# First modulation of a decoder trunk: half of its width on TensorE, with the condition's column as the stationary operand

## The chip, the core and the metric

The kernel runs on one core of one Trainium2 chip. The metric is the device time of one execution in microseconds; lower is better. A core has TensorE (PE, matrix products, with its weight loads PEld), VectorE (DVE), ScalarE (ACT), GpSimdE (POOL) and SyncE (SP, which issues most transfers). Each engine works through its own instructions in order and waits on semaphores of the others; 16 DMA engines move data between the chip's memory and the on-chip memory. A tile is a buffer of 128 partitions in the on-chip memory; a bank is a buffer of 128 x 512 values into which PE accumulates.

## What is computed

A trunk of two layers. The input x has 512 positions of width 1024, the condition c is one row of width 1024, and everything is in 32-bit floats. Each layer has three sub-layers (a gated feed-forward part, a mixer of attention and convolution, a second feed-forward part), and each of the six is fed by a norm that the condition modulates:

```
mod = (silu(c) @ w_ada[layer] + b_ada[layer]).reshape(b, N_SUB, N_MOD, D_MODEL)
shift = mod[:, :, 0, None, :]
scale = mod[:, :, 1, None, :]
gate = mod[:, :, 2, None, :]

def ada(z, i):
    return _rmsnorm(z, norm_g[layer, i]) * (1.0 + scale[:, i]) + shift[:, i]

x = x + 0.5 * gate[:, 0] * _swiglu(ada(x, 0), ffn_w1[layer, 0], ffn_w2[layer, 0])
...
```

The change touches only the first of these six modulations: shift and scale (2 x 1024 values) of layer 0, sub-layer 0. Nothing of the trunk's large products can start before some of them are there.

## The kernel before

The 1024 values of the width lie on 8 tiles x[0] to x[7] of 128 partitions (width) by 512 columns (positions). A modulation value belongs to one partition of one such tile, so DVE makes them in columns: cb holds silu(c) as a row repeated over all 128 partitions, a weight tile holds 128 rows of the transposed w_ada, and one instruction (ada_job, line 305) multiplies the two, 128 x 1024, and adds up along the row, which leaves 128 values of shift or of scale. For each of the 8 tiles j there is one job for shift and one for scale, 16 in all; ada_norm (lines 311 and 312) adds the bias and multiplies by the norm's gain for one range of tiles.

At the program's start (lines 980 to 1043) cb is made by two PE products of one row of ones with the two halves of c (line 1005) and a Silu on ACT (line 1006). The squares of x are summed (ACT line 403, DVE line 404), reduced by PE (line 410), turned into an inverse root by ten small DVE instructions, and spread over the partitions by four PE transposes (line 419). The result is called rb.

The first feed-forward part has its first eight weight products fed in an order of its own, side_by_side (lines 1019 to 1043). The width's 8 tiles are taken in 4 pairs k = 0 to 3. For a pair, the two jobs of each of its tiles, ada_norm, and then first.early make the first 256 positions (DVE line 438, ACT line 461, and the split into a high and a low half on ACT line 519 and DVE line 520), with which PE makes one step of 24 products (line 286). After k = 1 and k = 3 first.second makes the other 256 positions of two pairs, and PE makes two further steps of 24. That is 8 steps, 192 products of 128 x 128 by 256 columns. They need four weight tiles (raw), which ACT and DVE split into halves whi and wlo (lines 169 and 170). Then come the ordinary groups of the first feed-forward part, which begin with the tile called left.

The order in which an engine takes its instructions is set by a scheduler from the program's order and its priorities, so an instruction can stand earlier or later than the code suggests. Transfers stand in SP's queue in order: one that waits for its buffer holds up those behind it. The weights of this modulation (ada) have three buffers of 1 MB, each for shift and scale of one tile j.

Of the kernel before, what the change touches and what calls it, by code (L numbers as in the profile page):

```python
# [10 lines left out]
F32 = mybir.dt.float32  # L11
# [3 lines left out]
AF = mybir.ActivationFunctionType  # L15
# [93 lines left out]
def trunk(ctx: ExitStack, tc: tile.TileContext, t: dict):  # L109
# [8 lines left out]
    def acc_bank():  # L118
        return psum.tile([128, 512], F32, name="acc", tag="acc", bufs=6)
# [6 lines left out]
    def half_kb(name):  # L126
        return tmp.tile([128, S], F32, name=name, tag="ev", bufs=8)
# [175 lines left out]
    def ada_job(w, l, s, m, j):  # L303
        raw, _ = mods[l, s]
        nc.vector.scalar_tensor_tensor(w, w, 1.0, cb, op0=ALU.mult, op1=ALU.mult,  # L305
                                       accum_out=raw[:, m, j:j + 1])
# [677 lines left out]
    ada = []  # L984

    def load_ada():
        ada.append(sp.tile([128, 2, D], F32, name="ada", tag="ada", bufs=3))
        nc.sync.dma_start(ada[-1], t["w_ada"][0, 0:2 * KD].rearrange("(m j) p n -> j p m n", m=2)[len(ada) - 1])

    c = [half_kb("c")[0:1] for _ in range(2)]  # L990
    for half in range(2):
        nc.sync.dma_start(c[half], t["c"][:, half * 512:half * 512 + 512])
    load_ada()
    for j in range(KD):
        nc.sync.dma_start(x[j], t["xT"][j])
        if j == 3:
            nc.sync.dma_start(ident, t["ident"])
            nc.sync.dma_start(par, t["par"])
    load_ada()
    lead[:] = 0, 0, 0  # L1000
    fetch(4)
    for half in range(2):
        ps = acc_bank()
        cols = slice(half * 512, half * 512 + 512)
        nc.tensor.matmul(ps, row, c[half], start=True, stop=True)
        nc.scalar.activation(cb[:, cols], ps, AF.Silu)
    for m in range(2):
        ada_job(ada[0][:, m], 0, 0, m, 0)
    acc = sums()
    for j in range(KD):  # L1010
        squares(acc, j, slice(0, S))
    load_ada()
    load_ada()
    rb = spread(inv_rms(acc, 4), acc_bank())
    h = new_h()
    first = Blocks(0, 0, h, sp, first_tiles(sp))
    Tail.blocks[:] = [first]
# [1 line left out]
    def side_by_side(banks, done):  # L1019
        plain_groups = _ffn_order()[:4]  # L1020
        feeds = [Feed(0, 0, h, sum(plain_groups[i:i + 2], []), banks) for i in (0, 2)]
        for k in range(KD // 2):
            for j in (2 * k, 2 * k + 1):
                for m in range(2) if j else ():
                    ada_job(ada[j][:, m], 0, 0, m, j)
                if j and len(ada) < KD:
                    load_ada()
            ada_norm(0, 0, slice(2 * k, 2 * k + 2))
            first.early(rb[:, 0:256], k)
            feeds[0].step(k)  # L1030
            if k % 2:
                first.second(rb[:, 256:512], k // 2)
                feeds[1].step(k - 1)
                feeds[1].step(k)
        lead[:] = AHEAD, LOADED, SUMS
        for step in (first.t1, first.t2, first.t3):
            for two in range(2):
                after(LATER, lambda step=step, two=two: step(two))
        for group in plain_groups:
            for n, p in group:  # L1040
                done(n, p)
        release(True)
        late_constants()
# [26 lines left out]
def _laid_out(inp):  # L1070
    c = np.ascontiguousarray
    a = {k: np.asarray(v) for k, v in inp.items()}
    out = {}
    out["c"] = c(a["c"].reshape(1, D))
    out["xT"] = c(a["x"][0].T.reshape(KD, 128, S))
    out["w_ada"] = c(a["w_ada"].transpose(0, 2, 1).reshape(DEPTH, 72, 128, D))
    out["par"] = c(np.concatenate([
        a["b_ada"].reshape(DEPTH * 72, 128).T,
        a["norm_g"].reshape(DEPTH * 3 * KD, 128).T,
        a["conv_w"].reshape(DEPTH, 3, 4, 128).transpose(3, 0, 2, 1).reshape(128, 24),  # L1080
        a["conv_b"].reshape(DEPTH * 4, 128).T], axis=1))
    out["ident"] = np.eye(128, dtype=np.float32)
    out["mask"] = _mask()
    q, k = a["q_norm_g"], a["k_norm_g"]
    out["qkg"] = c(np.stack([q, q, k, k], axis=1).reshape(1, DEPTH * 4 * HD))
    w = a["w_in"]

    qkv = w[:, :, :1536].reshape(DEPTH, 4, 2, 128, 3, 4, 128)
    out["w_qkv"] = c(qkv.transpose(0, 5, 1, 3, 2, 4, 6).reshape(DEPTH, 4, 4, 128, 768))
    gcu = w[:, :, 1536:].reshape(DEPTH, KD, 128, 3, 4, 128)  # L1090
    out["w_gcu"] = c(gcu.transpose(0, 4, 3, 2, 1, 5).reshape(DEPTH, 4, 3, 128, D))
    wo = a["w_out"].reshape(DEPTH, KD, 128, KD, 128)
    wo = np.concatenate([wo[:, 4:], wo[:, :4]], axis=1)
    out["w_out"] = c(wo.transpose(0, 3, 2, 1, 4).reshape(DEPTH, KD, 128, D))

    w1 = a["ffn_w1"].reshape(DEPTH, 2, KD // 2, 2, 128, 2, NP, 2, 128)
    out["w1"] = c(w1.transpose(0, 1, 6, 5, 3, 4, 7, 2, 8).reshape(DEPTH, 2, NP, 4, 128, D))
    w2 = a["ffn_w2"].reshape(DEPTH, 2, NF, 128, KD, 128)
    wa = w2[:, :, :16].reshape(DEPTH, 2, 2, 8, 128, KD, 128)
    out["w2a"] = c(wa.transpose(0, 1, 2, 5, 4, 3, 6).reshape(DEPTH, 2, 2, KD, 128, D))  # L1100
    out["w2b"] = c(w2[:, :, 16:].transpose(0, 1, 4, 3, 2, 5).reshape(DEPTH, 2, KD, 128, 768))
    return out
# [17 lines left out]
```

## Time and profile before

| | us |
|---|---|
| median of three runs | 1890.41 (1887.54 to 1891.17) |
| the profiled execution | 1890.81 |
| its span | 1889.0 |
| PE busy | 1834.2 (97% of the span) |
| DVE busy | 1418.1 (75%) |
| ACT busy | 925.2 (49%) |

The span goes from the first to the last instruction in the profile; 1.8 us of the profiled execution lie outside it. The views used are the page of the whole execution, the timeline of one engine (start, duration, what it is, and in brackets how long the engine had been idle before it and what ended that), and a table of stretches with each engine's busy time.

### The profile page before, as it was taken

Reading aid. Unit: us, or ns where it says so; the run is one execution under the profiler, and the core shown is the slowest. Engines: PE = TensorE matmul, PEld = TensorE weight load, DVE = VectorE, ACT = ScalarE, POOL = GpSimd, SP = SyncE. Lnnn points to the kernel's source line nnn. Section 1 sums busy time; section 2 is a strip of 40 time slices with the busy share of each in tenths; the row PEclk is TensorE's granted clock in tenths of the full one; section 3 lists DMA queues with packets and bytes.
Section 4 is the critical chain, followed back from the end, with each engine's and each line's share of the span. In section 5 each row is a group of like instructions: output and inputs, shape, how many; then the busy total and the mean of one; then the engine's idle time right before and its main releaser. Section 6 shows DMA issues by size and latency. Waiting matters only on the chain.

```text
span 1889.0 us, 31142 instructions
## 1 busy us (share of the span) xinstructions
PE 1834.2 (97%) x12436; PEld 1702.1 (90%) x12436; DVE 1418.1 (75%) x2434; ACT 925.2 (49%) x1462; POOL 81.6 (4%) x156
## 2 busy tenths in 40 slices
PE   5899999999999999999989999999999999999999
PEld 4888999999988998998989999898998899989898
DVE  7887878787866887887778877766977768647564
ACT  3552543446653743543546435354656646436342
POOL 0000000000000000000000000000000000000000
PEclk9999999999999999999999999999999999999999
DMA  8678775522315278787725866723222245626422
GB/s 320 191 225 261 215 241 188 156 76 65 110 67 179 66 206 264 196 244 236 217 68 156 242 207 166 245 71 97 84 73 90 97 127 133 165 83 168 133 61 85
DMA packets 85124, 296.32 MB, mean 157 GB/s; under 512 B 9330, under 2 KB 10354, under 8 KB 84980
## 3 DMA queue, kind: packets, MB, share of 16 engines
q1 hardware_dynamic: 73460, 252.40, 38.9%
q0 software_dynamic: 11520, 41.95, 12.9%
q8 instruction: 97, 1.59, 0.3%
q14 instruction: 47, 0.39, 0.1%
HBM read 292.21 MB, written 2.10 MB: 156 GB/s over the span
## 4 chain that ended last, share of the span: by engine, by line
PE 81%; DVE 5%; ACT 3%; DMA 2%; issue 2%; ACTq 0%; DVEq 0%; POOLq 0%
PE acc L286 35%; PE acc L279 14%; PE acc L280 14%; PE acc L281 14%; DMA left<-in_w 2%; DVE wlo L170 1%; DVE h L520 1%; PE acc L873 1%; ACT whi L169 1%; PE tp L864 1%; PE tp L894 1%; DMA ada<-in_w_ada 1%; PE acc L904 0%; PE acc L905 0%; DVE p L908 0%
## 5 line engine op out<-in xcount | busy, mean ns | idle before, releaser
L286 PE MATMUL acc<-h,whi 128*128 128x256 f32 x4992 | 894.5, 282 | 28.6 <-ACT h L519 16.0
L286 PEld LDWEIGHTS acc<-h,whi 128*128 128x128 f32 x4992 | 770.2, 189 | 35.2 <-ACT h L519 18.0
L286 PE MATMUL acc<-h,wlo 128*128 128x256 f32 x2496 | 700.7, 281 | 0.4 <-DVE wlo L170 0.4
L169 ACT ACTIVATE whi<-raw 128x1024 fp32r<-128x1024 f32 (+1 forms) x304 | 306.0, 1011 | 372.3 <-PE acc L280 242.3
L286 PEld LDWEIGHTS acc<-h,wlo 128*128 128x128 f32 x2496 | 473.6, 190 | 1.1 <-DVE wlo L170 1.0
L170 DVE TENSOR_TENSOR wlo<-raw,whi 128x1024 fp32r<-128x1024 f32 (+1 forms) x304 | 352.5, 1166 | 52.9 <-ACT whi L169 49.9
L279 PE MATMUL acc<-hidh,whi 128*128 128x512 f32 (+1 forms) x776 | 287.4, 370 | 0.0
L281 PE MATMUL acc<-hidh,wlo 128*128 128x512 f32 (+1 forms) x776 | 287.0, 370 | 0.0
L280 PE MATMUL acc<-hidl,whi 128*128 128x512 f32 (+1 forms) x776 | 286.9, 370 | 0.0
L305 DVE SCALAR_TENSOR_TENSOR ada<-ada,cb 128x1024 f32<-128x1024 f32 x144 | 174.0, 1222 | 87.7 <-DMA ada<-in_w_ada 81.6
L536 DVE SCALAR_TENSOR_TENSOR x<-acc,fin,x 128x512 f32<-128x512 f32 (+1 forms) x130 | 87.6, 675 | 128.3 <-PE acc L281 128.1
L281 PEld LDWEIGHTS acc<-hidh,wlo 128*128 128x128 f32 x776 | 146.3, 189 | 24.8
L280 PEld LDWEIGHTS acc<-hidl,whi 128*128 128x128 f32 x776 | 146.4, 189 | 24.3
L279 PEld LDWEIGHTS acc<-hidh,whi 128*128 128x128 f32 x776 | 146.3, 189 | 24.3
L169 ACT ACTIVATE whi<-sum 128x1024 fp32r<-128x1024 f32 x80 | 84.8, 1061 | 147.0 <-DVE sum L222 100.7
L169 ACT ACTIVATE whi<-left 128x1024 fp32r<-128x1024 f32 x80 | 84.7, 1058 | 122.7 <-DMA left<-in_w 79.2
L170 DVE TENSOR_TENSOR wlo<-left,whi 128x1024 fp32r<-128x1024 f32 x80 | 97.7, 1221 | 52.6 <-ACT whi L169 52.1
L279 PE MATMUL acc<-h,whi 128*128 128x512 f32 (+1 forms) x346 | 132.1, 382 | 0.4 <-ACT h L519 0.4
L280 PE MATMUL acc<-h,whi 128*128 128x512 f32 (+1 forms) x346 | 126.9, 367 | 1.0 <-DVE h L520 1.0
L281 PE MATMUL acc<-h,wlo 128*128 128x512 f32 (+1 forms) x346 | 127.0, 367 | 0.0
L170 DVE TENSOR_TENSOR wlo<-sum,whi 128x1024 fp32r<-128x1024 f32 x80 | 97.7, 1221 | 32.5 <-ACT whi L169 32.3
L279 PE MATMUL acc<-whi,h 128*128 128x384 f32 x256 | 89.0, 349 | 4.8 <-ACT h L442 4.8
(123 smaller groups left out, 2148.4 us busy)
## 6 DMA issues: line engine op xcount, KB each, us to landing
ada<-in_w_ada SPq DMA_DIRECT2D x128, 512.0 KB, 4.4
raw<-in_w SPq DMA_DIRECT2D x96, 512.0 KB, 4.3
raw<-in_w2a SPq DMA_DIRECT2D x64, 512.0 KB, 5.0
left<-in_w SPq DMA_DIRECT2D x40, 512.0 KB, 4.4
sum<-in_w SPq DMA_DIRECT2D x40, 512.0 KB, 4.7
sum<-in_w POOLq DMA_DIRECT2D x40, 512.0 KB, 7.0
left<-in_w POOLq DMA_DIRECT2D x40, 512.0 KB, 5.4
raw<-in_w2b SPq DMA_DIRECT2D x32, 384.0 KB, 3.4
```

The source lines that it names most:

```text
L169: nc.scalar.activation(hi, raw, AF.Copy)
L170: nc.vector.tensor_tensor(out=lo, in0=raw, in1=hi.bitcast(F32), op=ALU.subtract)
L279: nc.tensor.matmul(out, a[0], b[0], start=first, stop=False)
L280: nc.tensor.matmul(out, a[0], b[1], start=False, stop=False)
L281: nc.tensor.matmul(out, a[1], b[0], start=False, stop=last)
L286: nc.tensor.matmul(out, p, q, start=first and i == 0, stop=i == 2, skip_group_check=True)
L305: nc.vector.scalar_tensor_tensor(w, w, 1.0, cb, op0=ALU.mult, op1=ALU.mult, accum_out=raw[:, m, j:j + 1])
L520: return nc.vector.tensor_tensor(out=lo, in0=v, in1=hi.bitcast(F32), op=ALU.subtract)
L536: nc.vector.scalar_tensor_tensor(x[j][:, cols], ps, gate, x[j][:, cols], op0=ALU.mult, op1=ALU.add)
L864: nc.tensor.transpose(pt[:, c * 128:(c + 1) * 128], p[:, c * 128:(c + 1) * 128], ident)
L873: nc.tensor.matmul(ps, v[c][:, i], z[:, c], start=c == m == 0, stop=c == n - 1 and m == 1)
L894: nc.tensor.transpose(ps[:, b * 128:(b + 1) * 128], qk[b][:, c], identr)
```

## The change

The weights of tiles 0 to 3 (shift and scale, 4 x 1 MB of ada before) are no longer laid out for DVE. A second layout, w_mod, holds w_ada's first 512 columns of shift and of scale with the condition's index on the partitions: 8 transfers of 128 x 1024, 0.5 MB each. The condition is also loaded as a 128 x 8 tile ccol, on which ACT makes Silu. PE takes one column of ccol as the stationary operand and 512 columns of weights as the moving one, 8 products in a row for scale (m = 1) and 8 for shift (m = 0), each set adding up in one row of 512 values. ACT copies the two rows out, PE turns each piece of 128 values into a column (8 products, line 1034 of the changed program), ACT copies these 8 columns into the modulation's tile, and one ada_norm covers tiles 0 to 3. Tiles 4 to 7 stay with DVE. The new weight tiles have four buffers, two of their own and two of the pool that later modulations use; ada has two buffers in place of three. The load of the four raw tiles stands behind the new loads in the program.

```
     def load_ada():
-        ada.append(sp.tile([128, 2, D], F32, name="ada", tag="ada", bufs=3))
-        nc.sync.dma_start(ada[-1], t["w_ada"][0, 0:2 * KD].rearrange("(m j) p n -> j p m n", m=2)[len(ada) - 1])
+        j = KD // 2 + len(ada)
+        ada.append(sp.tile([128, 2, D], F32, name="ada", tag="ada", bufs=2))
+        nc.sync.dma_start(ada[-1], t["w_ada"][0, 0:2 * KD].rearrange("(m j) p n -> j p m n", m=2)[j])
+    ccol = sp.tile([128, KD], F32, name="ccol")
+    nc.sync.dma_start(ccol, t["ccol"])
...
-    load_ada()
...
+    rows = {}
+    for m in (1, 0):
+        rows[m] = []
+        for k in range(KD // 2):
+            pool, name = ((sp, "adar"), (wp, "ada"))[k % 2]
+            rows[m].append(pool.tile([128, 1024], F32, name=name, tag=name, bufs=2).rearrange("p (i n) -> p i n", i=2))
+            nc.sync.dma_start(rows[m][-1], t["w_mod"][m, k])
+    nc.scalar.activation(ccol, ccol, AF.Silu)
     lead[:] = 0, 0, 0
-    fetch(4)
...
-    for m in range(2):
-        ada_job(ada[0][:, m], 0, 0, m, 0)
...
+    rb = spread(inv_rms(acc, 4), acc_bank())
+    flat = {}
+    for m in (1, 0):
+        ps = acc_bank()[0:1]
+        for k in range(KD):
+            nc.tensor.matmul(ps, ccol[:, k:k + 1], rows[m][k // 2][:, k % 2], start=k == 0, stop=k == KD - 1)
+        flat[m] = half_kb("row")[0:1]
+        nc.scalar.activation(flat[m], ps, AF.Copy)
+    fetch(4)
     load_ada()
     load_ada()
-    rb = spread(inv_rms(acc, 4), acc_bank())
+    ps = tp_bank()
+    for m in (1, 0):
+        for j in range(KD // 2):
+            nc.tensor.matmul(ps[:, m * 4 + j:m * 4 + j + 1], flat[m][:, j * 128:j * 128 + 128], row[:, 0:1],
+                             start=m == 1 and j == 0, stop=True, skip_group_check=True)
+    nc.scalar.activation(mods[0, 0][0][:, 0:2, 0:KD // 2], ps[:, 0:8].rearrange("p (m j) -> p m j", m=2), AF.Copy)
+    ada_norm(0, 0, slice(0, KD // 2))
...
         for k in range(KD // 2):
-            for j in (2 * k, 2 * k + 1):
-                for m in range(2) if j else ():
-                    ada_job(ada[j][:, m], 0, 0, m, j)
-                if j and len(ada) < KD:
-                    load_ada()
-            ada_norm(0, 0, slice(2 * k, 2 * k + 2))
+            if k > 1:
+                for j in (2 * k, 2 * k + 1):
+                    for m in range(2):
+                        ada_job(ada[j - KD // 2][:, m], 0, 0, m, j)
+                    if len(ada) < KD // 2:
+                        load_ada()
+                ada_norm(0, 0, slice(2 * k, 2 * k + 2))
```

PE's instructions from the product with the condition to the first large product, before the change:

```order
L1005 MATMUL acc_135<-c_93,row_82 128x512
L1005 MATMUL acc_138<-c_94,row_82 128x512
L410 MATMUL tp_170<-ones_80,ssq_143 128x1 x4
L419 MATMUL acc_195<-ident_77,sm_193 128x128 x4
L286 MATMUL acc_209<-h_200,whi_119 128x256
L286 MATMUL acc_210<-h_200,whi_127 128x256
```

PE's instructions from the spreading of rb to the first large product, after the change (adar and ada are here the tiles of w_mod):

```order
L419 MATMUL acc_180<-ident_77,sm_178 128x128 x4
L1025 MATMUL acc_185<-adar_109,ccol_93 1x512 x2
L1025 MATMUL acc_185<-ada_111,ccol_93 1x512 x2
L1025 MATMUL acc_185<-adar_113,ccol_93 1x512 x2
L1025 MATMUL acc_185<-ada_115,ccol_93 1x512 x2
L1025 MATMUL acc_196<-adar_117,ccol_93 1x512 x2
L1025 MATMUL acc_196<-ada_119,ccol_93 1x512 x2
L1025 MATMUL acc_196<-adar_121,ccol_93 1x512 x2
L1025 MATMUL acc_196<-ada_123,ccol_93 1x512 x2
L1034 MATMUL tp_235<-row_82,row_194 128x1 x4
L1034 MATMUL tp_235<-row_82,row_205 128x1 x4
L286 MATMUL acc_256<-h_247,whi_215 128x256
```

Between the spreading and the first large product stand now 16 products with the condition and 8 that turn rows into columns.

DVE's instructions from the end of the inverse root to the jobs of the second pair, before the change:

```order
L388 SCALAR_TENSOR_TENSOR sm_193<-sm_191,sm_183 128x4
L305 SCALAR_TENSOR_TENSOR ada_109,mod00_85<-ada_109,cb_67 128x1024 x2
L311 TENSOR_TENSOR fin00_86<-mod00_85,par_76 128x2x2
L312 SCALAR_TENSOR_TENSOR fin00_86<-fin00_86,par_76 128x2
L170 TENSOR_TENSOR wlo_120<-raw_111,whi_119 128x1024
L438 SCALAR_TENSOR_TENSOR z_219<-x1_69,fin00_86,acc_195 128x256
L438 SCALAR_TENSOR_TENSOR z_219<-x0_68,fin00_86,acc_195 128x256
L170 TENSOR_TENSOR wlo_124<-raw_113,whi_123 128x1024
L170 TENSOR_TENSOR wlo_128<-raw_115,whi_127 128x1024
L520 TENSOR_TENSOR h_200<-hva_202,h_200 128x2x256
L170 TENSOR_TENSOR wlo_132<-raw_117,whi_131 128x1024
L305 SCALAR_TENSOR_TENSOR ada_166,mod00_85<-ada_166,cb_67 128x1024 x2
```

The same place after the change:

```order
L388 SCALAR_TENSOR_TENSOR sm_178<-sm_176,sm_168 128x4
L170 TENSOR_TENSOR wlo_216<-raw_207,whi_215 128x1024
L170 TENSOR_TENSOR wlo_220<-raw_209,whi_219 128x1024
L170 TENSOR_TENSOR wlo_224<-raw_211,whi_223 128x1024
L170 TENSOR_TENSOR wlo_228<-raw_213,whi_227 128x1024
L311 TENSOR_TENSOR fin00_86<-mod00_85,par_76 128x2x4
L312 SCALAR_TENSOR_TENSOR fin00_86<-fin00_86,par_76 128x4
L438 SCALAR_TENSOR_TENSOR z_260<-x1_69,fin00_86,acc_180 128x256
L438 SCALAR_TENSOR_TENSOR z_260<-x0_68,fin00_86,acc_180 128x256
L438 SCALAR_TENSOR_TENSOR z_291<-x3_71,fin00_86,acc_180 128x256
L438 SCALAR_TENSOR_TENSOR z_291<-x2_70,fin00_86,acc_180 128x256
```

The jobs of tiles 0 to 3 are gone, all four low halves of the weights stand ahead of the modulation's end (fin), and the first job that is left stands behind the start of pairs 0 and 1.

SP's transfers behind those of x, after the change (raw are the four weight tiles of the first products):

```order
L1009 DMA ada_115<-in_w_mod 128x1024 [waits DMAHW0_49]
L162 DMA raw_207<-in_w1 128x1024 [waits DMAHW1_49]
L162 DMA raw_209<-in_w1 128x1024 [waits DMAHW2_49]
L1009 DMA adar_117<-in_w_mod 128x1024 [waits DMAHW5_49,DMAHW3_49,PE_49]
L1009 DMA ada_119<-in_w_mod 128x1024 [waits DMAHW6_49,DMAHW4_49,PE_49]
L1009 DMA adar_121<-in_w_mod 128x1024 [waits DMAHW7_49,PE_49]
L1009 DMA ada_123<-in_w_mod 128x1024 [waits DMAHW0_49,PE_49]
L162 DMA raw_211<-in_w1 128x1024
L162 DMA raw_213<-in_w1 128x1024
L990 DMA ada_231<-in_w_ada 128x2x1024 [waits DMAHW1_49]
```

The four tiles of w_mod for shift wait until PE has used those for scale, and two of the four raw tiles stand behind them.

## Rows read from the trace of the kernel before

**Rows 1.** The page's head, span of the profiled execution

```profile
span 1889.0 us, 31142 instructions
```

**Rows 2.** Stretches: start:end, length, busy us of each engine (count), PEclk, DMA share

```profile
0.00:25.00 25.00, 6.73 (x16) 3.65 (x16) 15.76 (x35) 12.10 (x18) 0.20 (x4) 1.00 0.92 355
25.00:60.00 35.00, 29.76 (x195) 28.40 (x195) 29.19 (x59) 13.87 (x28) 1.87 (x2) 0.90 0.86 315
60.00:140.00 80.00, 71.69 (x574) 69.47 (x574) 68.58 (x85) 44.45 (x61) 6.11 (x7) 0.98 0.65 180
```

**Rows 3.** Timeline of PE: start, us, what, [idle before <-what ended it]

```profile
2.17 3.74 PE L1005 MATMUL acc<-c,row 1*128 1x512 f32 x4 [2.17 <-DMA c<-in_c]
14.41 1.87 PE L410 MATMUL tp<-ones,ssq 128*128 128x1 f32 x8 [8.50 <-DVE ssq L404]
18.31 1.12 PE L419 MATMUL acc<-ident,sm 128*128 128x128 f32 x4 [2.03 <-DVE sm L388]
25.08 1.38 PE L286 MATMUL acc<-h,whi 128*128 128x256 f32 x3 [5.65 <-ACT h L519]
...
34.63 1.30 PE L286 MATMUL acc<-h,whi 128*128 128x256 f32 x3 [3.69 <-ACT h L519]
...
50.55 0.50 PE L286 MATMUL acc<-h,whi 128*128 128x256 f32 x2 [1.23 <-ACT h L519]
```

**Rows 4.** Timeline of ACT: Silu of the condition, a high half of weights

```profile
4.24 0.60 ACT L1006 ACTIVATE cb<-acc 128x512 f32<-128x512 f32 x1 [2.22 <-PE acc L1005]
5.95 0.60 ACT L1006 ACTIVATE cb<-acc 128x512 f32<-128x512 f32 x1 [1.11 <-PE acc L1005]
...
24.93 1.04 ACT L169 ACTIVATE whi<-raw 128x1024 fp32r<-128x1024 f32 x1
```

**Rows 5.** Timeline of PE around 40 and 45 us: two pitches of equal products

```profile
40.22 0.63 PE L286 MATMUL acc<-h,whi 128*128 128x256 f32 x2
40.65 0.41 PE L286 MATMUL acc<-h,wlo 128*128 128x256 f32 x1
...
44.75 0.28 PE L286 MATMUL acc<-h,wlo 128*128 128x256 f32 x1
44.87 0.40 PE L286 MATMUL acc<-h,whi 128*128 128x256 f32 x2
45.10 0.28 PE L286 MATMUL acc<-h,wlo 128*128 128x256 f32 x1
```

**Rows 6.** Stretches of 2 us around the clock's changes (PEclk is the third number from the end)

```profile
40.00:42.00 2.00, 2.00 (x14) 2.00 (x14) 2.00 (x3) 0.00 (x0) 0.00 (x0) 0.72 0.85 289
...
76.00:78.00 2.00, 2.00 (x11) 2.00 (x11) 1.78 (x3) 1.58 (x2) 0.00 (x0) 0.50 1.00 246
```

**Rows 7.** Timeline of DVE: jobs, sums of squares, weight halves, fin and the modulated tiles

```profile
6.60 1.23 DVE L305 SCALAR_TENSOR_TENSOR ada<-ada,cb 128x1024 f32<-128x1024 f32 x1 [5.58 <-ACT cb L1006]
...
8.89 1.48 DVE L404 TENSOR_TENSOR ssq<-ssq,sq 128x512 f32<-128x512 f32 x2
...
20.86 1.23 DVE L170 TENSOR_TENSOR wlo<-raw,whi 128x1024 fp32r<-128x1024 f32 x1
...
28.29 1.22 DVE L305 SCALAR_TENSOR_TENSOR ada<-ada,cb 128x1024 f32<-128x1024 f32 x1
...
29.44 1.22 DVE L305 SCALAR_TENSOR_TENSOR ada<-ada,cb 128x1024 f32<-128x1024 f32 x1
...
32.05 0.16 DVE L312 SCALAR_TENSOR_TENSOR fin<-fin,par 128x2 f32<-128x2 f32 x1
...
33.03 1.65 DVE L438 SCALAR_TENSOR_TENSOR tv<-x,fin,acc 128x256 f32<-128x256 f32 x4
...
36.37 1.32 DVE L520 TENSOR_TENSOR h<-tv,h 128x512 fp32r<-128x512 f32 x2
```

**Rows 8.** The page's DMA issues: a 0.5 MB transfer, median us from issue to landing

```profile
left<-in_w SPq DMA_DIRECT2D x40, 512.0 KB, 4.4
```

**Rows 9.** Timeline of PE: the squares' reduction once more, late in the first layer

```profile
959.75 0.50 PE L410 MATMUL tp<-ones,ssq 128*128 128x1 f32 x4
```

More of the change, by code (lines that the diff above doesn't have):

```diff
@@ L1022, in side_by_side @@
         for k in range(KD // 2):
-            for j in (2 * k, 2 * k + 1):
-                for m in range(2) if j else ():
-                    ada_job(ada[j][:, m], 0, 0, m, j)
-                if j and len(ada) < KD:
-                    load_ada()
-            ada_norm(0, 0, slice(2 * k, 2 * k + 2))
+            if k > 1:
[5 more added lines that the diff above has]
+                ada_norm(0, 0, slice(2 * k, 2 * k + 2))
             first.early(rb[:, 0:256], k)
@@ L1076, in _laid_out @@
     out["w_ada"] = c(a["w_ada"].transpose(0, 2, 1).reshape(DEPTH, 72, 128, D))
+    wm = a["w_ada"][0, :, :2 * D].reshape(KD // 2, 2, 128, 2, D)[..., :S]
+    out["w_mod"] = c(wm.transpose(3, 0, 2, 1, 4))
+    out["ccol"] = c(a["c"].reshape(KD, 128).T)
     out["par"] = c(np.concatenate([
```

## The prediction

> **What bounds the kernel now.** I read the page's head first, then a table of stretches, then the timelines of PE, DVE and ACT over the first 60 us. The profiled execution took 1890.81 us, of which the span is 1889.0 [rows 1]; I reckon against this execution, which stands 0.4 us above the median. PE is busy nearly all the time, so what the start costs is time in which PE can't yet multiply. In the first 25 us PE is busy for 6.7 us and from 25 to 60 us for 29.8 of 35 [rows 2]. The change lives wholly in these 60 us. PE's timeline has three marks [rows 3]: the first large product at 25.08 us, the second pair's at 34.63 after 3.69 us of idle time, the last pair's (k = 3) at 50.55 after 1.23 us. All three waits end with h, the modulated tile, so DVE's chain of jobs, fin, z and split is what PE waits for, and the 8 jobs of tiles 0 to 3 that the change removes are on it. A job takes 28.29 to 29.44, 1.15 us [rows 7]; eight are 9.2 us. That is the most that could be gained. From the last pair's first product on, 72 products remain, and after them the ordinary groups start. Those 72 are the same before and after. So I forecast when the last pair's first product comes, and take its shift as the shift of the end.
>
> **PE's new work, and when it starts.** The 16 products with the condition stand in PE's queue behind the four transposes that spread rb. Before, these begin at 18.31 and last 1.12, to 19.43 [rows 3]. Two jobs stood ahead of the sums of squares on DVE, which begin at 8.89 [rows 7]; without them the first sum waits for ACT, whose second Silu still ends at 6.55 [rows 4] and is followed by one square of the same size (0.6, and 0.1 to start), so 7.25. That is 1.6 us earlier, and x itself comes earlier because 1 MB of ada no longer goes ahead of it. Start: 19.4 - 1.6 = 17.8. The four tiles for scale follow x directly and the others wait only for PE, so data are no bound at the start: 2 MB of x and 2 MB of w_mod take the place of 2 MB of ada, 2 of x and 2 of raw that were on chip by some 25 us.
>
> The price of one product: plain 32-bit floats, 512 moving columns. The trace has this type twice, in the product that spreads c. The two Silu that wait for it start at 4.24 and 5.95 [rows 4], so one product takes 1.71 us; both together take 3.74 [rows 3]. PE ran at 1.2 GHz there: the large products of 256 columns that follow at 25 us still come 0.21 us apart, as at 40.22 to 40.65 (two in 0.43), while three take 0.35 at 44.75 to 45.10 [rows 5]. The clock column shows the change between the two, 0.72 in 40 to 42 us [rows 6]; it reads 1.00 before its first recorded change, and there the pitch decides. The price halves with the clock: the squares' reduction takes 1.87 for 8 records at the start [rows 3] and 0.50 for 4 late in the layer [rows 9], 0.23 against 0.125 each. So a product costs 1.71 at 1.2 GHz and 0.86 at 2.4 GHz, and 16 of them 27.4 or 13.7 us. The stationary operand here is one column and there 128; I take the price as that of the moving side, since its 512 columns are the same.
>
> The Trainium skill (TensorE: Matmul & The Clock Gate, Back-to-back issue gap) gives the gap as the number of moving columns over the clock, 0.43 us for 512 at 1.2 GHz. The row shows four times that for this type, and the row decides; by the page's gap 16 products would be an estimated 6.8 us, which is the third rival below.
>
> **When the clock rises.** The clock column's 0.72 in 40 to 42 us is 0.50 up to about 41.1 and 1.00 from there: PE had then multiplied for 6.5 us since 34.63 [rows 3, 6]. The 16 products come back to back too. Does a stream with one stationary column raise the clock? No row shows such a stream. I take the nearest rows, the large products, and 6.5 us counted from the transposes, which start 1.1 ahead of the first product: 5.4 after it. Then 3.2 products run at 1.71 and 12.8 at 0.86: 5.4 + 11.0 = 16.4, the end is at 34.2. The other bound, no rise at all, gives 17.8 + 27.4 = 45.2.
>
> **From the last product to the modulated tile.** The second row's copy on ACT takes some 0.6 (as Silu on 512 columns, [rows 4]) and 0.1 to start. Behind it ACT has the fourth tile's high half, 1.04 [rows 4], and DVE that tile's low half, 1.23 [rows 7], ahead of fin. The 8 turning products cost two records each like those of line 410, 8 x 0.25 = 2.0 at 2.4 GHz or 8 x 0.47 = 3.8 at 1.2, plus 0.35 for the copy that follows. So fin starts 3.0 after the last product at full clock (the weights' halves are later) or 4.15 at half (the turning is), and takes 0.4. From fin's last instruction, 32.05 + 0.16, to the pair's first product at 34.63 [rows 3, 7] it is 2.4. First large product: 34.2 + 3.0 + 0.4 + 2.4 = 40.0, or 45.2 + 4.15 + 0.4 + 2.4 = 52.1 without the rise. Before it was 25.08.
>
> The transfers behind: two of the four raw tiles stand in SP's queue behind the tiles for shift, which wait for PE. The last of these goes out when PE ends scale, at about 27.3; a transfer of this size lands 4.4 later [rows 8], so the raw tiles land by 33, before the 34.2. This is hidden; if each landed 2 us later, it would show in full.
>
> **From there to the last pair.** DVE now has pairs 0 and 1 at once, then the jobs of pair 2. From fin on: 8 tiles at 0.41 (four in 1.65), 4 splits at 0.65 (two in 1.32) [rows 7], 4 jobs at 1.15 and 0.5 of waits and small ones, 11.0 us to the next fin; the pair's two tiles and split, 2.7; 4 jobs of pair 3, 4.6; fin 0.4; to the product 2.4. Together 21.1, or 18.7 from the first large product (2.4 after fin). PE needs for its 120 products before that 14.1 at 0.1175 each, or some 2.5 more if it lost its clock in the gap of over 3 us before (the clock column shows 0.50 in 76 to 78 us, after a pause, [rows 6]). Both are under 18.7, so this stretch is DVE's and the clock costs nothing. Before, the same way took 50.55 - 25.08 = 25.5: here are 6.8 us that the change gains.
>
> **The sum.** Last pair: 40.0 + 18.7 = 58.7 against 50.55, later by 8.1. 1890.8 + 8.1 = **1899 us**. The first product is 14.9 later and 6.8 come back. If PE idles long enough ahead of the last pair to lose its clock, up to 3 more are due; PE's idle time between 60 and 140 us is 8.3 [rows 2], and a part of 1 to 5 us may vanish, since transfers then have a lead. For this case alone 1894 to 1903.
>
> **Rivals.** (1) The clock doesn't rise on a one-column stream. The first large product is at 52.1, the last pair's at 70.8, later by 20.2: 1911, with 1908 to 1914 around it. For it: such a stream fills one of 128 columns of PE, and no row shows it lifting the clock. Against: PE reads as many rows and columns as in any product, and the unbroken stream from 34.63 us did [rows 3, 6]. [...]
>
> (2) The delay is absorbed. PE's 8.3 us of idle time between 60 and 140 us would have to be ends of transfers that don't move with PE. If over 4.3 of them go, the sum is within 0.2%, some 1892. Against: PE's waits there are for ACT and DVE, which work on what PE frees.
>
> (3) The one-column product is cheap: no dearer per column than the large products, whose 256 columns take 0.21 us at 1.2 GHz [rows 5], so 0.43. Then the tiles for shift are the bound: PE ends scale at 21.2, the last tile lands by 26, the last raw by 28, its halves end at 30.4, the first product is at 33 and the last pair's at 51.9: 1892, no change. It decides from a price under 0.5. Against: the type's own row.
>
> That PE doesn't take these products over at all isn't open: the order shows them in its queue.
>
> **Chances.** Forecast 0.54, rival 1 0.38, rival 2 0.05, rival 3 0.03. The first two are slower. A measurement of this kernel tells about 0.2%, 3.8 us, from no change. Slower 0.92, same 0.06, and 0.02 for faster, the far ends of rivals 2 and 3. The range takes in the forecast's and rival 1's cases, 1893 to 1914.
>
> **What would show it.** On PE: 16 products between the transposes and the first large one, 16.4 us in all with a step from 1.71 to 0.86 (27.4 without one: rival 1; under 8: rival 3); a first large product near 40 us; the last pair's 18.7 later, with DVE as what ended the wait. On DVE: idle time of some 15 us before fin, then no gap. If PE reaches the last pair with no wait, the 18.7 is wrong. If the shift at the last pair isn't the shift at the end, the stretch from 60 to 140 us has it.

## The result and the profile after the change

| | before | after |
|---|---|---|
| median of four runs each, taken side by side, us | 1890.79 (1887.54 to 1891.38) | 1904.86 (1903.19 to 1907.54) |
| span of the profiled execution, us | 1889.0 | 1903.7 |
| first large product, us | 25.08 | 40.55 |
| first product of the last pair, us | 50.55 | 61.35 |
| ACT begins with the tile left, us | 57.58 | 70.19 |

The changed kernel is slower: the ratio of the times is 1.0081, with a 95% interval of 1.0066 to 1.0095, some 14 to 15 us. The last row is a mark for the end of the start: ACT begins the high half of left there, after a wait that PE's first large products end. It is called the left mark below; before the change it comes 57.58 - 50.55 = 7.03 us after the last pair's first product.

PE's timeline of after, the rows that answer to [rows 3] (start, us, what, in brackets the idle time before and what ended it):

```profile
16.94 1.11 PE L419 MATMUL acc<-ident,sm 128*128 128x128 f32 x4 [2.04 <-DVE sm L388]
17.99 3.57 PE L1025 MATMUL acc<-adar,ccol 128*1 128x512 f32 x4
21.35 2.08 PE L1025 MATMUL acc<-ada,ccol 128*1 128x512 f32 x4
23.27 1.88 PE L1025 MATMUL acc<-adar,ccol 128*1 128x512 f32 x4
...
32.04 1.88 PE L1025 MATMUL acc<-ada,ccol 128*1 128x512 f32 x4
33.85 1.05 PE L1034 MATMUL tp<-row 1*128 1x1 f32 x8
35.63 1.05 PE L1034 MATMUL tp<-row 1*128 1x1 f32 x8 [0.73 <-ACT row L1027]
40.55 1.31 PE L286 MATMUL acc<-h,whi 128*128 128x256 f32 x3 [3.88 <-ACT h L519]
61.35 0.80 PE L286 MATMUL acc<-h,whi 128*128 128x256 f32 x2 [3.94 <-ACT h L519]
```

Each row of line 1025 is two products (two records each). The first two take 3.36 us, the next two 1.92, and from 23.27 on two take 1.72: 1.68 and 0.86 for one. All 16 take 33.85 - 17.99 = 15.9 us. The rest of the delay stands in DVE's timeline, from the weights' low halves to the last pair's fin:

```profile
35.13 1.23 DVE L170 TENSOR_TENSOR wlo<-raw,whi 128x1024 fp32r<-128x1024 f32 x1 [13.95 <-ACT whi L169]
36.55 1.23 DVE L170 TENSOR_TENSOR wlo<-raw,whi 128x1024 fp32r<-128x1024 f32 x1 [0.20 <-ACT whi L169]
37.69 0.16 DVE L311 TENSOR_TENSOR fin<-mod,par 128x8 f32<-128x8 f32 x1
...
53.60 1.23 DVE L305 SCALAR_TENSOR_TENSOR ada<-ada,cb 128x1024 f32<-128x1024 f32 x1 [1.93 <-DMA ada<-in_w_ada]
...
56.15 1.23 DVE L305 SCALAR_TENSOR_TENSOR ada<-ada,cb 128x1024 f32<-128x1024 f32 x1 [0.17 <-DMA ada<-in_w_ada]
...
58.56 0.16 DVE L311 TENSOR_TENSOR fin<-mod,par 128x4 f32<-128x4 f32 x1
```

DVE, the engine that the change relieves, is idle 13.95 us and later waits 1.93 + 0.17 us for weights of ada. SP's timeline (issues) shows why:

```profile
27.28 0.90 SPq L162 DMA_DIRECT2D raw<-in_w  x2
28.22 1.56 SPq L990 DMA_DIRECT2D ada<-in_w_ada  x2
...
46.13 2.67 SPq L990 DMA_DIRECT2D ada<-in_w_ada  x2
```

The loads of the two ada buffers go out from 28.2 us on; the third and fourth go out at 46.1, when DVE has finished with the first. And PE's 3.94 us of idle time ahead of the last pair cost the clock, in stretches of 2 us (PE first, PEclk third from the end):

```profile
56.00:58.00 2.00, 1.40 (x12) 1.20 (x11) 1.85 (x3) 0.00 (x0) 0.00 (x0) 1.00 1.02 416
58.00:60.00 2.00, 0.00 (x0) 0.00 (x0) 1.90 (x7) 0.53 (x2) 0.00 (x0) 0.82 1.03 422
60.00:62.00 2.00, 0.65 (x2) 0.50 (x2) 2.00 (x5) 2.00 (x6) 0.87 (x1) 0.50 1.02 414
...
64.00:66.00 2.00, 2.00 (x11) 2.00 (x11) 0.40 (x1) 0.60 (x1) 0.00 (x0) 0.50 1.04 274
66.00:68.00 2.00, 2.00 (x19) 2.00 (x18) 0.69 (x1) 0.00 (x0) 0.00 (x0) 0.97 0.97 211
```

The last pair's products run at 1.2 GHz up to 66 us, 10 or 11 in 2 us where 19 fit later. Here the left mark is 70.19 - 61.35 = 8.84 us behind the last pair, 1.81 more than before.

### The profile page after: what moved, and what is told of

Its sections match the earlier page's. It is cut to its first block, busy times and chain, and to the rows that moved or that the text cites. A ratio compares the mean times of both kernels' runs of the same rounds, so it can differ in the third digit from the quotient of the medians.

```text
span 1903.7 us, 31230 instructions
## 1 busy us (share of the span) xinstructions
PE 1852.8 (97%) x12484; PEld 1708.3 (90%) x12484; DVE 1408.7 (74%) x2416; ACT 926.1 (49%) x1466; POOL 81.6 (4%) x156
## 4 chain that ended last, share of the span: by engine, by line
PE 58%; DVE 2%; ACT 1%; DMA 1%; issue 1%; ACTq 0%
PE acc L286 29%; PE acc L279 9%; PE acc L280 9%; PE acc L281 9%; DMA left<-in_w 1%; DVE h L520 1%; PE acc L873 0%; PE tp L864 0%; PE tp L894 0%; DVE wlo L170 0%; ACT whi L169 0%; PE acc L905 0%; PE acc L904 0%; DVE p L908 0%; DVE z L438 0%
## 5 line engine op out<-in xcount | busy, mean ns | idle before, releaser
L305 DVE SCALAR_TENSOR_TENSOR ada<-ada,cb 128x1024 f32<-128x1024 f32 x136 | 164.7, 1223 | 82.5 <-DMA ada<-in_w_ada 82.3
```

## The experiments

Eight kernels were run. The marks of all are from their timelines (us). The ratio is to the kernel before in the same group of runs, whose median there was 1889.73 for three_ada, raw_first, half_products and no_products, 1890.90 for both_loads and second_pair, and 1891.34 for filled_gap and raw_ahead:

| kernel | first large product | last pair | left mark | mark minus last pair | median | ratio, 95% interval |
|---|---|---|---|---|---|---|
| before | 25.08 | 50.55 | 57.58 | 7.03 | 1890.79 | |
| after | 40.55 | 61.35 | 70.19 | 8.84 | 1904.86 | 1.0081 (1.0066 to 1.0095) |
| three_ada | 40.42 | 58.50 | 65.54 | 7.04 | 1898.79 | 1.0049 (1.0034 to 1.0064) |
| raw_first | 40.70 | 56.94 | 63.98 | 7.04 | 1898.27 | 1.0051 (1.0031 to 1.0070) |
| both_loads | 40.81 | no wait | 63.25 | | 1899.10 | 1.0042 (1.0029 to 1.0054) |
| half_products | 37.94 | 60.03 | 68.67 | 8.64 | 1902.63 | 1.0070 (1.0055 to 1.0085) |
| no_products | 25.22 | 46.06 | 54.43 | 8.37 | 1887.30 | 0.9986 (0.9976 to 0.9996) |
| filled_gap | 40.97 | 62.02 | 69.06 | 7.04 | 1902.80 | 1.0053 (1.0036 to 1.0070) |
| second_pair | 28.80 | 52.33 | 59.37 | 7.04 | 1897.43 | 1.0038 (1.0025 to 1.0052) |
| raw_ahead | 31.37 | 48.95 | 55.97 | 7.02 | 1893.04 | 1.0012 (1.0000 to 1.0023) |

In both_loads PE runs into the last pair without a wait, and no row marks its start. The fifth column has two kinds of values: 7.02 to 7.04 where PE waited 1.23 us or less ahead of the last pair, and 8.4 to 8.8 in the three kernels where it had waited 3.9 us or more.

**no_products: what PE's products cost as a whole.** The changed kernel without the two matrix parts:

```
-    for m in (1, 0):
-        ps = acc_bank()[0:1]
-        for k in range(KD):
-            nc.tensor.matmul(ps, ccol[:, k:k + 1], ...)
-        ...
-    for m in (1, 0):
-        for j in range(KD // 2):
-            nc.tensor.matmul(ps[:, m * 4 + j:m * 4 + j + 1], ...)
-    nc.scalar.activation(mods[0, 0][0][:, 0:2, 0:KD // 2], ps[:, 0:8]..., AF.Copy)
+    nc.scalar.activation(mods[0, 0][0][:, 0:2, 0:KD // 2], ccol..., AF.Copy)
```

> The changed kernel without the 16 products and the turning; the modulation's values of tiles 0 to 3 are put there by one small copy of other numbers, so this part of the computation is left out; all loads stay, but none waits for PE. It shows what the change could give if PE did its part for nothing. Theory: all of x, the condition's weights and raw land by about 24 us, the first large product comes at 25 to 26 us as before the change, the last pair's about 20 us later (45 to 46 in place of 50.55), and the time is 1885 to 1888, under that of before by 3 to 5 us. Rival (the loss lies in the start's transfers or behind the start): the time stays at 1895 or above.

PE's timeline of this kernel, its waits ahead of the large products:

```profile
25.22 0.80 PE L286 MATMUL acc<-h,whi 128*128 128x256 f32 x2 [7.08 <-ACT whi L169]
...
46.06 1.30 PE L286 MATMUL acc<-h,whi 128*128 128x256 f32 x3 [4.00 <-ACT h L519]
```

It came as expected. The ratio is 0.9986 against 1.0081: the products with their turning, and the loads that wait for them, are worth 0.95%, some 18 us. And with this half of the modulation free, at no cost to PE at all, the kernel is 0.14% faster than the kernel before. More the change can't give with these loads: the first large product stays at 25.22, now behind the weights' halves (whi), and the 9.2 us of DVE's jobs bring the last pair only 4.5 us forward (50.55 to 46.06). DVE still waits 2.0 us for the ada loads, and behind PE's 4.00 us of idle time the mark takes 8.37 in place of 7.03; what it would be with three ada buffers was not tried.

**half_products: how the delay goes with their number.** Every second product is left out (8 of 16):

```
-        for k in range(KD):
-            nc.tensor.matmul(ps, ..., start=k == 0, stop=k == KD - 1)
+        for k in range(0, KD, 2):
+            nc.tensor.matmul(ps, ..., start=k == 0, stop=k == KD - 2)
```

> The changed kernel with every second product with the condition left out (8 in place of 16): the modulation of tiles 0 to 3 is then summed over half of the condition only, everything else is as it was, and every weight tile is still loaded and used. Theory (the price of these products sets the first large product): 8 products end near 27 us in place of 33.9; then the raw tiles, whose loads go out when the shift tiles' have gone (about 23 us), are last and land near 30, so the first large product comes at 36 to 37, 4 us earlier, and the time falls by 4 to 5 us, to about 1900. Rival (the products hide behind the transfers): the first large product stays within 1 us of 40.55.

The first large product came 2.6 us earlier, and the ratio is 0.1% lower, no more than the two intervals leave open; both are less than was expected. PE's timeline shows a part of what took over, a wait for the last tile of the condition's weights:

```profile
30.45 1.02 PE L1025 MATMUL acc<-ada,ccol 128*1 128x512 f32 x2 [1.67 <-DMA ada<-in_w_mod]
```

ACT's timeline shows the rest:

```profile
31.50 0.59 ACT L1027 ACTIVATE row<-acc 1x512 f32<-1x512 f32 x1 [6.49 <-PE acc L1025]
32.00 1.04 ACT L169 ACTIVATE whi<-raw 128x1024 fp32r<-128x1024 f32 x1
...
33.30 1.05 ACT L169 ACTIVATE whi<-raw 128x1024 fp32r<-128x1024 f32 x1
...
35.61 1.04 ACT L169 ACTIVATE whi<-raw 128x1024 fp32r<-128x1024 f32 x1
```

Three weight tiles are still to be halved when the products end, the last of them behind fin; so behind the products lies a second bound, the weights' halves, of nearly the same height. At the other end PE waited 4.72 us ahead of the last pair, and the clock fell again (8.64).

**raw_first and three_ada: the loads.** In raw_first the four raw tiles are loaded ahead of the tiles for shift. In three_ada the third ada buffer is back, and the w_mod tiles that had buffers of their own borrow from a pool that is used only later:

```
@@ raw_first
     for m in (1, 0):
+        if m:
+            for i in range(4):
+                loaded[i] = load_unit(*order[i])
@@ three_ada
-        ada.append(sp.tile([128, 2, D], F32, name="ada", tag="ada", bufs=2))
+        ada.append(sp.tile([128, 2, D], F32, name="ada", tag="ada", bufs=3))
...
-            pool, name = ((sp, "adar"), (wp, "ada"))[k % 2]
+            pool, name = ((sum_pool[0], "sum"), (wp, "ada"))[k % 2]
```

> The changed kernel with all four raw weight tiles loaded ahead of the shift tiles of the condition's weights, so that none of them waits behind PE. Theory (PE's products end last): the 16 products still end at 33.9, the turning into columns still follows, and the first large product moves by no more than 1.3 us from 40.55. Rival (the two raw tiles that landed at 34 us are what the start waits for): the first large product comes 4 to 6 us earlier and the time falls as much, to 1899 to 1901. In either case two jobs of tile 4 can run ahead of the modulation's end on DVE, which shortens the stretch to the last pair by some 2 us.

> The changed kernel with three buffers for the weights of tiles 4 to 7 again (ada); room for them comes from taking two buffers of the pool called sum for the condition's weights, which stand idle at that time. In the changed kernel the third of these loads was issued only at 46.1 us, when DVE had freed a buffer, and DVE waited 1.9 us for it ahead of pair 3. Theory (the late load lengthens the stretch to the last pair): the wait of 1.9 goes, the last pair's first product comes at about 59.2 in place of 61.35, and as PE then idles under 2 us before it in place of 3.9, the clock may stay up, another 1.8: the time falls by 2 to 4 us, to 1901 to 1903. Rival (the loss comes from the 16 products alone, and what follows moves with the first large product): the first large product stays at 40.5 and the time stays within 1 us of 1904.9.

The first large product stays where it was in both (40.70 and 40.42), so the rival with 4 to 6 us of waiting for the raw tiles is out. They do hold up the start of fin, by 0.9 us: in raw_first fin begins at 36.80 in place of 37.69, and then a job of tile 4 stands between its two instructions, which takes that up again:

```profile
36.80 0.17 DVE L311 TENSOR_TENSOR fin<-mod,par 128x8 f32<-128x8 f32 x1 [0.26 <-ACT mod L1039]
36.88 1.22 DVE L305 SCALAR_TENSOR_TENSOR ada<-ada,cb 128x1024 f32<-128x1024 f32 x1
...
38.03 0.16 DVE L312 SCALAR_TENSOR_TENSOR fin<-fin,par 128x4 f32<-128x4 f32 x1
```

But the last pair is 4.4 and 2.85 us earlier, and the ratios fall by 0.30% and 0.32%, some 6 us each, more than was expected of three_ada (2 to 4). PE's timelines, raw_first:

```profile
56.94 0.50 PE L286 MATMUL acc<-h,whi 128*128 128x256 f32 x2 [0.21 <-ACT h L519]
```

and three_ada:

```profile
58.50 0.50 PE L286 MATMUL acc<-h,whi 128*128 128x256 f32 x2 [0.90 <-ACT h L519]
```

The wait of 3.94 us has become 0.21 and 0.90. In three_ada DVE no longer waits for ada. In raw_first two jobs of the third pair (tile 4) stand ahead of fin's end, the first of them in DVE's idle time. In both the clock stays up, and the distance to the left mark is back at 7.04.

**both_loads: do the two add up?** Both edits together.

> The changed kernel with both cures of its loads: the raw tiles ahead of the tiles for shift, and a third ada buffer. By the theory each took away the same wait (DVE's for ada ahead of the last pair, and with it PE's idle time and the fall of the clock), so they don't add up: the last pair is at 56 to 57, the left mark at 63 to 64.5 (57.58 before the change), the time 1896 to 1898.5, still slower than before by 6 to 8. Rival (two separate losses, 6 us each): they add up, and the time is 1891 to 1893, close to the kernel before.

They don't. The left mark is at 63.25, 0.7 ahead of raw_first's, and the time, 1899.10, is not better (it is 0.6 above the expected range). From 46 to 58 us PE is busy without a gap (stretches of 2 us of this kernel, the first and the last of six):

```profile
46.00:48.00 2.00, 2.00 (x20) 2.00 (x19) 2.00 (x6) 0.00 (x0) 0.00 (x0) 1.00 0.99 276
...
56.00:58.00 2.00, 2.00 (x20) 2.00 (x19) 0.99 (x3) 1.72 (x4) 0.00 (x0) 1.00 1.02 338
```

So with the loads mended, what is left is the first large product at 40.8 and PE's own work behind it. None of the three ways of loading that were tried gets this kernel back to the time before.

**filled_gap: the price of the lost clock.** 28 products whose result is not used, in PE's idle time ahead of the last pair:

```
             first.early(rb[:, 0:256], k)
+            if k == 3:
+                ps = tp_bank()
+                for i in range(28):
+                    nc.tensor.matmul(ps[:, 0:256], feeds[0].ws[0][0][:, 256:384],
+                                     moving(h, 2, feeds[0].group[0][1])[0], start=i == 0, stop=i == 27)
             feeds[0].step(k)
```

> The changed kernel with 28 further products of 256 columns, whose result nobody uses, between the step of the third pair and that of the last pair: 28 x 0.1175 = 3.3 us of work in PE's 3.94 us of idle time ahead of the last pair (57.4 to 61.35). By the theory that this idle time cost PE its full clock, the last pair still comes at 61.2 to 61.6, since DVE sets it, but its products come 0.1175 apart from the start: the left mark (70.19) is 1.5 to 2.4 earlier, 67.8 to 68.7, and the time 1902.5 to 1903.4. Rival, as the prediction had it (the clock costs nothing, DVE sets this too): the left mark stays at 70 and the time at 1905.

PE's timeline:

```profile
57.55 3.46 PE L1057 MATMUL tp<-h,whi 128*128 128x256 f32 x28
62.02 0.50 PE L286 MATMUL acc<-h,whi 128*128 128x256 f32 x2 [1.01 <-ACT h L519]
```

The last pair came 0.7 later (62.02, outside the expected range), since DVE sets it and both had waited longer for transfers, PE 1.00 us for a tile of the condition's weights and DVE 0.25 us more for ada. But from there to the left mark it takes 7.04 instead of 8.84: up to this mark the idle time as such cost nothing, and the clock that it took cost 1.8.

The lead of 1.1 us at the left mark doesn't last. Some 18 us behind it PE waits 2.3 us for ACT in both kernels (2.33 in the changed kernel, 2.31 here), as it does in the kernel before (2.26, at 75.14 us). Stretches of 8 us around this wait, of the kernel before, the changed kernel and filled_gap:

```profile
74.00:82.00 8.00, 6.86 (x45) 6.86 (x46) 6.09 (x10) 4.32 (x7) 0.06 (x1) 0.79 0.81 194
```

```profile
86.00:94.00 8.00, 6.11 (x49) 5.92 (x50) 7.53 (x11) 5.97 (x9) 0.72 (x1) 1.00 0.80 167
```

```profile
86.00:94.00 8.00, 7.26 (x47) 7.13 (x47) 6.08 (x9) 4.32 (x8) 0.44 (x1) 0.79 0.79 197
```

The clock falls behind it in filled_gap, and before the change too, but not in the changed kernel. ACT's next two evictions (copies of what PE has summed up in a bank to the tile ev), in the same order:

```profile
81.84 1.07 ACT L651 ACTIVATE ev<-acc 128x512 f32<-128x512 f32 x2
```

```profile
93.05 1.07 ACT L651 ACTIVATE ev<-acc 128x512 f32<-128x512 f32 x2
```

```profile
93.43 1.07 ACT L651 ACTIVATE ev<-acc 128x512 f32<-128x512 f32 x2
```

Here the changed kernel is 11.2 us behind the kernel before, 1.4 less than at its left mark, and filled_gap is 0.4 behind the changed kernel. The same holds in all profiled executions: in the three kernels that had lost the clock ahead of the last pair (the changed kernel, half_products, no_products) it stays up behind this wait, and in the seven others it falls. So the 1.8 is a price up to the left mark, of which 0.4 is left at 82 us against the kernel before. The median is 2.1 us below that of the changed kernel (1902.80), but the intervals of the two ratios overlap, and the trace does not tie this difference to the unused products.

**second_pair and raw_ahead: a version that would beat both.** Before the change PE has 5.65 us of idle time ahead of the first large product. Here PE takes the second pair alone (tiles 2 and 3), so that the 16 products have 256 columns; DVE keeps the first pair ahead of them, and there are three ada buffers:

```
+    tiles = [0, 1, 4, 5, 6, 7]
...
+    for m in (1, 0):
+        ps = acc_bank()[0:1, 0:256]
+        for k in range(KD):
+            nc.tensor.matmul(ps, ccol[:, k:k + 1], rows[m][k // 4][:, k % 4], start=k == 0, stop=k == KD - 1)
+        nc.scalar.activation(flat[:, m * 256:m * 256 + 256], ps, AF.Copy)
...
-            for j in (2 * k, 2 * k + 1):
+            for j in (2 * k, 2 * k + 1) if k != 1 else ():
```

> PE takes only the second pair (tiles 2 and 3): 16 products of 256 columns in place of 512; DVE keeps the jobs of tiles 0 and 1 ahead of them as before the change, and those of tiles 4 to 7. Three ada buffers; the 4 weight tiles for PE (2 MB) need no wait and go ahead of the raw tiles. By the theory (the price goes by moving columns, 0.86 us per product at 1.2 GHz and 0.43 at 2.4, and they stand between the transposes at 18 to 19 us and the first pair's tile, in time in which PE had nothing to do before): the products end near 28, beside DVE's weight halves; the first large product is at 27.5 to 29.5 (25.08 before the change), the second pair follows at once, since DVE has 4 jobs fewer, and the last pair is at 44 to 46 (50.55 before). The mark of the left tile, 57.58 before, is 3 to 5 earlier: 1884 to 1888. Rival (the transfers are the bound): 2 MB ahead of the raw tiles in place of 2 MB of ada behind them put the first product at 30 or later, and the last pair's jobs wait for their ada tiles: no gain, 1889 or more.

It missed: the last pair is at 52.33 in place of 44 to 46, the left mark at 59.37, the time 0.38% above the kernel before. The products took 28.27 - 19.90 = 8.4 us, half of the 15.9 for half the columns, as expected, and the first large product came at 28.80. But ACT's timeline shows a jam:

```profile
24.92 0.37 ACT L1033 ACTIVATE row<-acc 1x256 f32<-1x256 f32 x1 [11.38 <-PE acc L1032]
...
26.66 1.04 ACT L169 ACTIVATE whi<-raw 128x1024 fp32r<-128x1024 f32 x1
```

The row's copy waits for PE with the weights' halves queued behind it; before the change the first high half was made at 17.15. DVE's low halves came late in turn, and its jobs with them. In raw_ahead only the loads differ, raw ahead of w_mod, with which the scheduler puts the halves first:

```
     load_ada()
+    lead[:] = 0, 0, 0
+    fetch(4)
     rows = {}
...
     nc.scalar.activation(ccol, ccol, AF.Silu)
-    lead[:] = 0, 0, 0
-    fetch(4)
```

> The kernel in which PE takes only the second pair (16 products of 256 columns), with one difference from the last such run: the four raw tiles go ahead of PE's weight tiles. There ACT stood 11.4 us before the copy of the first row, with the weights' high halves queued behind it (the first at 26.66 us, 17.15 before the change). By the theory that this is what spoiled it, ACT and DVE now halve all four raw tiles by 25 to 26 us, DVE does tile 4's two jobs ahead of the second pair, and the last pair (50.55 before the change, near 52 in that run) is at 45 to 47; the left mark (57.58 before, 59.37 in that run) is at 53 to 55.5, the time 1885 to 1888.5, that is 2 to 5 under the kernel before. Rival (PE's 8.4 us of new products ahead of the first large one are the cost, wherever the loads stand): the left mark stays at 58 to 60, and the time at 1893 to 1898.

The jam is gone (the high halves are made at 16.94 to 21.84), but PE's products now wait 2.25 us for their weights and end at 30.8. The left mark is at 55.97, 1.6 ahead of the kernel before, which is less than expected (53 to 55.5); the time is not ahead: 1.0012 (1.0000 to 1.0023) in place of 1885 to 1888.5. The gain is first given back at 124 us. ACT's timeline of raw_ahead there, and that of the kernel before:

```profile
119.25 1.06 ACT L169 ACTIVATE whi<-left 128x1024 fp32r<-128x1024 f32 x1 [4.88 <-DMA left<-in_w]
```

```profile
119.28 1.06 ACT L169 ACTIVATE whi<-left 128x1024 fp32r<-128x1024 f32 x1 [3.55 <-DMA left<-in_w]
```

and PE's, which waits for what ACT does behind it, again raw_ahead first:

```profile
124.72 0.80 PE L286 MATMUL acc<-h,whi 128*128 128x256 f32 x2 [3.90 <-ACT ev L651]
```

```profile
124.75 0.50 PE L286 MATMUL acc<-h,whi 128*128 128x256 f32 x2 [2.38 <-ACT ev L651]
```

PE arrives 1.55 us earlier and goes on at the same time: the transfer that POOL issues to add two weight tiles was issued 1.35 us earlier (112.33 against 113.68) and landed at the same time, 6.9 us later in place of 5.6. Why it took longer was not tried. Behind this wait the clock fell as well, which it did not before; the stretch in raw_ahead:

```profile
124.00:128.00 4.00, 3.28 (x15) 3.28 (x16) 3.85 (x6) 2.10 (x4) 0.00 (x0) 0.57 1.01 303
```

and before:

```profile
124.00:128.00 4.00, 3.25 (x28) 3.25 (x29) 3.88 (x6) 2.42 (x5) 0.00 (x0) 1.00 0.98 275
```

15 products in place of 28. This isn't the whole of it: compared one by one with the kernel before, ACT's evictions are 1.5 us late at 129 us, 0.8 ahead at 141, 2.0 ahead at 207, and 1.1 late at 252; at the end they are 1.5 late. What takes the lead between 207 and 252 us is open. So none of the versions that compute everything beats the kernel before.

## Why the prediction was right, and where not

The forecast was 1899 us, with 1893 to 1914 as the range, and slower at 0.92; it came to 1904.86. The direction and the main cause held, and the time is 6 above the likeliest value, outside that case's own 1894 to 1903; the range held it only because it took in the first rival's case too, which did not come. By its steps:

- **The start of PE's products** (17.8): 17.99. **The price** (1.71 and 0.86): 1.68 and 0.86. A product of half the columns (second_pair) costs half, so the price goes by the moving columns, as assumed, and one stationary column costs what 128 do (1.68 and 1.71). The third rival, a price under 0.5, is out. The Trainium skill (TensorE: Matmul & The Clock Gate, Back-to-back issue gap) gives the columns over the clock plus 2.5 ns at 2.4 GHz, an estimated 0.22 us for 512 columns; the rows show four times that for this type, and the rows decide.
- **The clock's rise** (5.4 us after the first product): the pitch changes at about 21.7, 3.7 us after it. A stream with one stationary column does lift the clock, and the first rival is out. All 16: 15.9 us for 16.4. That these agree so well is partly luck, since the rise doesn't come at a fixed time: raw_first's first two products take 2.64 us (18.20 to 20.84) and the next two 1.71, so it came within the first two, while half_products' first three take 1.66, 1.70 and 1.71 each, so it came only after 5.1 us.
- **From the last product to the first large one** (34.2 to 40.0): 33.85 to 40.55. The 3.0 us to fin were 3.8 (37.69): the third raw tile landed at 34.0, 6.8 us after its issue in place of the 4.4 taken from [rows 8], and ACT halved two weight tiles around the row's copy. At most 0.9 us hangs on this: with the raw tiles there in time (raw_first) fin begins at 36.80, though PE's products end 1 us later, behind the row that is turned in between.
- **18.7 us to the last pair: the step that failed.** It was 20.8. The sum had DVE's work right but left out that ada has two buffers in place of three, though the change says so: the third load leaves only when DVE has freed a buffer, 46.1, and DVE waited 1.93 + 0.17 = 2.1 us for it and the fourth, the whole difference. three_ada took this away: the last pair came 2.85 earlier, 7.95 behind the kernel before where the forecast said 8.1, and the time is 9.1 above that of the kernel before (1898.79 against 1889.73).
- **"This stretch is DVE's and the clock costs nothing": wrong in its second half.** "If PE idles long enough ahead of the last pair to lose its clock, up to 3 more are due" stood there as a reserve. By the prediction's own numbers PE would idle 18.7 - 14.1 - 2.5 = 2.1 us there, since the clock had been lost in the gap before (it was, up to 45.5 us); it idled 3.94 because DVE waited for ada. So this follows from the step above: in three_ada, without that wait, PE idles 0.90 and keeps the clock. It cost 1.8 up to the left mark (filled_gap, and the table's fifth column), and 1.4 of this was back at 82 us, since the kernel before lost the clock there and the changed one did not.
- **The end.** The prediction took the last pair's shift as that of the end, which holds only roughly. At the last pair the shift is 10.8, at the left mark 12.6 = 10.8 + 1.8 (clock), at the end 14.7. ACT's evictions, compared one by one with the kernel before, show that it goes up and down in between: 11.2 us late at 82 us (time of the kernel before), 13.8 at 129, 11.7 at 141, 10.2 at 207, 13.0 at 252 and 15.0 from 1585 on. Ahead of 129 lies the wait at 124 us named above, 2.38 us before and 3.13 after the change, and behind it the clock falls (0.50 from 138 to 140 us), where it stayed up before; but those 2 us are gone again at 141. From 1025 to 1029 us the clock falls once more in the changed kernel (0.57 on the mean) and not before, and its evictions are 1.5 us later behind it. So of the 3.5 us that come behind 82 us only a part is located, and why they come is open. The other kernels wander likewise: from the left mark to the last eviction their shift changes by -1.2 to +4.8 us.
- **The second rival** (a delay absorbed between 60 and 140 us) is out: of 12.6 us at the left mark 11.7 are there at 141, and PE is busy for 70.29 us in this stretch against 71.69 before [rows 2], so its idle time did not shrink.

```profile
0.00:25.00 25.00, 13.67 (x29) 4.84 (x30) 9.25 (x22) 9.39 (x14) 0.20 (x4) 1.00 0.69 241
25.00:60.00 35.00, 27.77 (x157) 19.85 (x155) 21.04 (x44) 10.82 (x22) 1.00 (x1) 0.89 0.94 344
60.00:140.00 80.00, 70.29 (x546) 68.10 (x547) 64.10 (x82) 46.13 (x65) 6.09 (x7) 0.95 0.62 167
```

These are the stretches of after that answer to [rows 2]: DVE has 6.5 us less to do in the first and 8.2 less in the second, PE 6.9 more in the first, and from 25 to 60 us PE has 2 us less, because its products can't start.

## What to carry to other kernels

Work that is moved to the engine that waits is free only if it fits into that engine's wait: 5.65 us were there, 15.9 went in, and the first large product moved by the rest and by what follows the last of them. When a change takes a buffer away, follow the load that needs it to its issue and its landing before adding up what is relieved. And where TensorE will wait some microseconds ahead of dense work, put the slower products into the sum, but follow the clock through the next waits too, in both kernels: here most of such a loss was made up at the next wait.

## What the runs showed of the hardware

- A stream of products with one stationary column lifted the clock, 3.7 us after its first product in the changed kernel, within the first 2.64 us in raw_first and after 5.1 us in half_products.
- The same wait of PE, some 120 to 137 us into the run, left the clock up in some kernels and not in others: it stayed at 1.00 behind 2.38 us (before) and 2.36 (no_products), and fell to 0.50 behind 2.07 (raw_first), 2.29 (filled_gap) and 3.13 (after). A fall made ACT's evictions behind it 1.3 to 1.6 us later. Unused products in the wait ahead of the last pair kept the clock up there, and it fell at the next wait (2.31 us) instead.
- A transfer that adds to a tile on its way, issued by POOL, landed 5.6 us after its issue in one kernel and 6.9 in another, at the same moment of the run.
